# A diffusion block with two layers on one core: new costs and a new order for its instruction planner, modulation sums by narrow products, one copy less in single-group norms

## The chip, the cores and the metric

The kernel runs on one core of a Trainium2 chip: TensorE (matrix products), VectorE, ScalarE, GpSimd and SyncE (which issues all transfers here). The metric is device time in microseconds of one execution.

## What is computed

Two layers of a block with modulation on 512 latent tokens and 256 context tokens, all 1024 wide, in fp32. In each layer the six modulation vectors for the latent and the context tokens come from one 1024x6144 matrix; the mixer has three parts (neighborhood attention, latent attention, a linear recurrence), and a gated feed-forward part follows. The second layer leaves the context tokens as they are.

```python
def _adaln(cvec, w, b):
    m = jax.nn.silu(cvec) @ w + b
    return jnp.split(m[:, None, :], 6, axis=-1)
...
for l in range(DEPTH):
    sh_m, sc_m, g_m, sh_f, sc_f, g_f = _adaln(c, ada_w[l], ada_b[l])
    csh_m, csc_m, cg_m, csh_f, csc_f, cg_f = _adaln(c_ctx[None], ada_w[l], ada_b[l])
    u = _modulate(_rmsnorm(h, norm_mix_g[l]), sh_m, sc_m) @ w_in[l]
    ...
    o_lat = jnp.concatenate([na_o.reshape(B, S, NA_WIDTH), mla_o.reshape(B, S, MLA_HEADS * MLA_V), lru_o], axis=-1)
    h = h + g_m * (o_lat @ w_out[l])
    h = h + g_f * _swiglu(_modulate(_rmsnorm(h, norm_ffn_g[l]), sh_f, sc_f), ffn_w_gate[l], ffn_w_up[l], ffn_w_down[l])
```

## The kernel before

Activations lie with the feature on the partitions: eight tiles of 128 features by 768 tokens. Each fp32 product is made of three: weight and activation are split into a rounded high part and the rest (`whi`, `wlo`; tiles `s`), and high x high, high x rest and rest x high are added up in PSUM (`lin`). With 768 tokens each goes out in a piece of 512 columns and one of 256, so that one block of 128 features takes six products, "a beat" in what follows; in the second layer's feed-forward part only 512 tokens are left and a beat is three products. Weights come by `load_w` (tiles `wst`, then split). Some products stay in plain fp32; the trace has two records for each of those.

**The order.** No instruction is issued where it stands. Helpers (`mm` L497, `tr` L506, `act`, `copy` L524, `tt` L535, `ts` L541, `stt`, `scan` L1298) hand each operation to `Order.add` (L246) with a cost in ns for each engine that may do it. `Order.place` (L304) then lays all of them out greedily while the kernel is built: again and again it takes, over all engines, the operation with the earliest start by the model, ties broken by rank (its place in the program plus shifts). Waits between engines (`HOPS`), a bias for each engine (`BIAS`), a clock model for TensorE (`ClockGate`) and free buffers go into that start. The result is the static order of each engine's queue. Within a mixer the steps are listed by hand in `PLAN` (L57 on), and each has an offset on its rank after "@" (`LEAD`): a first list for layer 0, a second for layer 1. SyncE issues its transfers in that order too, and one that waits for a buffer holds back those behind it.

**Modulation.** `ada_chunks(l, ch, nv)` (L698) makes chunks of 256 columns of the modulation matrix for `nv` vectors (latent and context, or latent alone). Eight transfers of 128x256 bring the chunk's weights into `ast` tiles (three buffers). For the first vector VectorE multiplies by the vector's entry (one per partition) and accumulates in `acc` (`stt`, L570); for the second, GpSimd scales the same tile (L544) and adds it (L537). The sum over the 128 partitions is taken by TensorE: each `acc` (as moving side, 256 columns) against a block of ones with 32 columns, four sums one beside the other in four column groups; the result is copied out, and two "closing" products with a selecting matrix turn it to the partitions again. `later` gives this work a shift of `FILL_LATE`, so that it fills gaps; `od.gate` holds its transfers until the last operation before it in the list is placed. In the first layer's mixer (`ada_rest`, L895) stand 12 chunks for two vectors, in its feed-forward part (L1332) 12 more for two and 16 for one.

**Norms.** `rstd` (L647) sums squares by a product with 32 columns, moves the sums to the partitions by transposes, raises them to the power of -1/2 on GpSimd (L670, tile `rn`), copies the results out to 128 columns a tile (`rb`) and transposes that back to PSUM, where VectorE reads it. It is called with one group (the whole width) in `norm_stat`, `latent_kv`, `latent_rope` and `latent_q`, and with two in `near_k`, `near_q`, `latent_k` and `latent_query`.

In the trace the first mixer lies at about 80 to 490 us, the first feed-forward part to about 1085, the second mixer at about 1125 to 1440 and the second feed-forward part from 1480 on.

## Time and profile before

| | us |
|---|---|
| three runs: median (lowest to highest) | 1846.58 (1841.27 to 1848.17) |
| profiled execution, its own time | 1840.35 |
| its span, first to last instruction | 1838.3 |
| TensorE busy | 1773.1 |
| VectorE busy | 1100.5 |
| GpSimd busy | 725.2 |
| ScalarE busy | 481.4 |

In the rows, PE is TensorE's products, PEld its weight loads, DVE VectorE, ACT ScalarE, POOL GpSimd, SP SyncE. An operation is told as out<-in by tile names; a product's inputs are moving side, then weight; "128*32" is rows by columns of the weight. Products overlap in the pipeline, so the length of one says less than the distance from its start to the start of the next. Idle time stands in brackets with what ended it.

### The profile page before, as it was taken

How to read it: one execution, taken by the hardware profiler on the slowest of the kernel's cores; microseconds unless marked ns; L12 is line 12 of the kernel's file. 1: busy time of each engine (PE TensorE's matmuls, PEld its weight loads, DVE VectorE, ACT ScalarE, POOL GpSimd, SP SyncE). 2: the span in 40 equal slices, each digit the busy share in tenths (PEclk: the TensorE clock that was granted, in tenths of full speed). 3: DMA queues.
4: the chain of work that ended last, by engine and by line, in shares of the span. 5: the costliest groups of instructions: out<-in, count | busy, mean ns of one | idle time of the engine just before them, and what ended most of it. 6: DMA issues, size and time to landing. Idle time of an engine off the chain costs nothing.

```text
span 1838.3 us, 25772 instructions
## 1 busy us (share of the span) xinstructions
PE 1773.1 (96%) x9880; PEld 1411.0 (77%) x9880; DVE 1100.5 (60%) x1850; ACT 481.4 (26%) x912; POOL 725.2 (39%) x698
## 2 busy tenths in 40 slices
PE   8999998899989999999999999999999999999999
PEld 4777765667778888888888887777677878888787
DVE  7765478897576566566634357676876644343443
ACT  4454264663130000000000013654664210000000
POOL 2333467777537766310121022335453122232322
PEclk9999999999999999999999999999999999999999
DMA  8111111224223343444422131111101223323233
GB/s 312 52 53 46 35 50 56 92 93 129 71 94 112 112 125 116 137 153 160 142 78 70 52 109 59 62 53 53 59 24 44 72 89 94 98 86 104 81 99 96
DMA packets 86380, 166.53 MB, mean 91 GB/s; under 512 B 9968, under 2 KB 51312, under 8 KB 86256
## 3 DMA queue, kind: packets, MB, share of 16 engines
q1 hardware_dynamic: 86256, 164.88, 28.3%
q8 instruction: 78, 1.28, 0.3%
q14 instruction: 46, 0.38, 0.1%
HBM read 160.65 MB, written 4.19 MB: 90 GB/s over the span
## 4 chain that ended last, share of the span: by engine, by line
PE 77%; DVE 11%; POOL 3%; issue 3%; DMA 3%; ACT 2%; SPq 0%; DVEq 0%; POOLq 0%; ACTq 0%
PE A L502 62%; PE B L502 10%; PE B L507 4%; DMA ast<-in_ada_dram 2%; DVE acc L570 2%; DVE s L537 1%; POOL rn L670 1%; DVE s L529 1%; DVE wlo L537 1%; POOL acc L537 1%; ACT lo L516 1%; DVE lo L570 1%; DVE whi L529 1%; DVE lo L1300 1%; DVE tmp L537 1%
## 5 line engine op out<-in xcount | busy, mean ns | idle before, releaser
L502 PE MATMUL A<-s,whi 128*128 128x512 f32 (+1 forms) x4340 | 1144.8, 355 | 8.3 <-DVE s L537 2.7
L502 PEld LDWEIGHTS A<-s,whi 128*128 128x128 f32 x4340 | 759.8, 189 | 160.4 <-issue 16.6
L502 PE MATMUL A<-s,wlo 128*128 128x512 f32 (+1 forms) x2138 | 735.7, 354 | 0.1
L502 PEld LDWEIGHTS A<-s,wlo 128*128 128x128 f32 x2138 | 395.9, 189 | 58.0 <-issue 8.0
L529 DVE CAST whi<-wst 128x1024 fp32r<-128x1024 f32 (+2 forms) x183 | 125.8, 688 | 407.4 <-PE A L502 355.6
L537 POOL TENSOR_TENSOR wlo<-wst,whi 128x640 fp32r<-128x640 f32 (+2 forms) x75 | 143.8, 1917 | 428.4 <-DVE whi L529 365.7
L570 DVE SCALAR_TENSOR_TENSOR acc<-ast,cc,acc 128x256 f32<-128x256 f32 x280 | 177.7, 635 | 99.7 <-DMA ast<-in_ada_dram 96.8
L516 ACT ACTIVATE tmp<-A 128x768 f32<-128x768 f32 (+1 forms) x75 | 55.2, 735 | 535.8 <-PE A L502 530.6
L537 DVE TENSOR_TENSOR wlo<-wst,whi 128x1024 fp32r<-128x1024 f32 (+2 forms) x133 | 164.0, 1233 | 6.9 <-POOL whi L531 1.9
L670 POOL TENSOR_TENSOR rn<-rn,con 128x12 f32<-128x12 f32 (+4 forms) x44 | 84.5, 1921 | 181.1 <-DVE rn L544 174.0
L537 POOL TENSOR_TENSOR acc<-acc,ast 128x256 f32<-128x256 f32 x168 | 139.5, 831 | 9.9
L544 POOL TENSOR_SCALAR ast<-ast,cc 128x256 f32<-128x256 f32 x168 | 108.8, 650 | 73.8 <-DVE acc L570 69.2
L502 PE MATMUL A<-s,s 128*128 128x512 f32 (+1 forms) x508 | 124.4, 353 | 13.8 <-ACT lo L516 9.2
L502 PE MATMUL B<-s,s 128*64 128x256 f32 (+2 forms) x720 | 110.6, 353 | 1.3 <-DVE s L529 1.3
L502 PEld LDWEIGHTS A<-s,s 128*128 128x128 f32 x508 | 81.0, 191 | 38.1 <-ACT lo L516 12.9
L507 PE MATMUL B<-ident,tmp 128*128 128x128 f32 (+1 forms) x480 | 78.9, 278 | 19.5 <-ACT tmp L527 11.1
L502 PE MATMUL B<-s,whi 128*128 128x512 f32 (+1 forms) x364 | 93.4, 344 | 0.0
L507 PEld LDWEIGHTS B<-ident,tmp 128*128 128x128 f32 (+1 forms) x480 | 56.6, 142 | 42.3 <-ACT tmp L527 13.4
L502 PEld LDWEIGHTS B<-s,s 128*64 128x64 f32 (+1 forms) x720 | 59.2, 144 | 28.4 <-issue 13.2
L531 POOL TENSOR_SCALAR s<-tmp 128x512 fp32r<-128x512 f32 (+2 forms) x24 | 29.5, 1229 | 127.0 <-DVE tmp L537 114.0
L527 ACT COPY s<-B 128x384 f32<-128x384 f32 (+2 forms) x149 | 67.5, 472 | 38.7 <-PE B L507 35.4
L531 POOL TENSOR_SCALAR whi<-wst 128x1024 fp32r<-128x1024 f32 (+4 forms) x24 | 25.5, 1064 | 122.0 <-PE A L502 73.9
(171 smaller groups left out, 1760.5 us busy)
## 6 DMA issues: line engine op xcount, KB each, us to landing
ast<-in_ada_dram SPq DMA_DIRECT2D x320, 128.0 KB, 2.1
wst<-in_wg_dram SPq DMA_DIRECT2D x44, 512.0 KB, 3.5
wst<-in_wu_dram SPq DMA_DIRECT2D x44, 512.0 KB, 3.6
wst<-in_win_dram SPq DMA_DIRECT2D x32, 512.0 KB, 3.5
wst<-in_wd_dram SPq DMA_DIRECT2D x32, 384.0 KB, 3.1
wst<-in_wd_dram SPq DMA_DIRECT2D x32, 320.0 KB, 2.9
wst<-in_wout_dram SPq DMA_DIRECT2D x16, 512.0 KB, 3.6
hr<-in_x_dram SPq DMA_DIRECT2D x16, 384.0 KB, 3.8
```

Of the source, the lines that this page charges most:

```text
L502: od.add({"t": c / 2.4}, lambda e: nc.tensor.matmul(ap(out), lhsT=ap(lhsT), rhs=ap(rhs), start=start, stop=stop), [out], [lhsT, rhs], heat ...
L507: od.add({"t": 256 / 2.4}, lambda e: nc.tensor.transpose(ap(out), ap(in_), ap(ident)), [out], [in_, ident])
L516: nc.scalar.activation(ap(out), ap(in_), getattr(AF, func), scale=ap(scale), **kw)
L527: nc.scalar.copy(out=ap(out), in_=ap(in_))
L529: nc.vector.tensor_copy(ap(out), ap(in_))
L531: nc.gpsimd.tensor_scalar(out=ap(out), in0=ap(in_), scalar1=1.0, scalar2=1.0, op0=ALU.mult, op1=ALU.mult)
L537: (nc.vector if e == "v" else nc.gpsimd).tensor_tensor(out=ap(out), in0=ap(a), in1=ap(b), op=op)
L544: (nc.vector if e == "v" else nc.gpsimd).tensor_scalar(out=ap(out), in0=ap(a), scalar1=ap(s1), scalar2=ap(s2), op0=op0, **kw)
L570: lambda e: nc.vector.scalar_tensor_tensor(out=ap(out), in0=ap(a), scalar=ap(s), in1=ap(b), op0=op0, op1=op1),
L670: lambda e: nc.gpsimd.tensor_tensor(out=ap(r[:, :w]), in0=ap(r[:, :w]), in1=ap(C("mhalf", 0, w)), op=ALU.pow),
L1300: lambda e: nc.vector.tensor_tensor_scan(out=ap(out), data0=ap(a), data1=ap(u), initial=ap(init), op0=ALU.mult, op1=ALU.add), [out], refs( ...
```

## The change

The planner's model changes in six ways: costs of products, transposes and scans get new figures; a product whose shape differs from the one before (fp32 with fewer than 128 weight columns, or at most 64 rows, or neither) costs `SWITCH` = 95 ns and is put behind others by as much; operations of VectorE that use two inputs in SBUF or a copying mode are marked `both`, and such an operation and any of GpSimd exclude each other in the model; the bias of GpSimd goes from -274 to +600; the rule by which late work may take a PSUM buffer is loosened a little. Both mixers' lists are ordered anew. In `ada_chunks` the scaling for the second vector and the first step may go to any of three engines and the addition to VectorE or GpSimd; each `acc` is now the weight (two halves of 128 columns) against a single column of ones, two products a sum, and VectorE adds the bias straight from PSUM for each chunk. In `rstd` with one group the copy falls away: the transposes read one column of `rn` with a step of zero as a weight of 128 columns.

```diff
 PLAN, LEAD = [], {}
 for _text in ("""
-    lru_start @-26, lru_in 0 @6, lru_in 1 @18, lru_gates 1 @-5, latent_rope @-58, latent_kv @561,
...
+    near_q 1 @-103, lru_in 1 @-1458, lru_in 0 @777, latent_rope @-15, lru_gates 1, latent_kv @-21, near_k 1 @-30,
+    lru_gates 0 @-1644, latent_v, latent_k 0, lru_out 0 @2414, near_q 0 @-1471, lru_out 1 @302, latent_keys,
+    latent_q @-2498, near_v 1, lru_start, latent_k 1 @25, near_q 2 @145, near_v 0 @176, lru_scan 0 @-92,
+    ada_rest @1227, lru_scan 1 @-2483, latent_query 1 @-183, latent_put 0, near_v 2 @-2500, latent_query 0 @-2218,
...
@@ Order.place
+        shape = 0
+        port = {"v": (0.0, 0.0), "g": (0.0, 0.0)}
...
-                        if w != j and (w < 0 and not b.loose or not b.psum or len(tg.free) <= j + 1):
+                        if w != j and (w < 0 and not b.loose or not b.psum or
+                                       not b.loose and len(tg.free) <= j + 1):
...
+                    if e == "g" or e == "v" and op.both:
+                        a, b = port["v" if e == "g" else "g"]
+                        if a <= st < b:
+                            st = b
                     if op.table is not None and e == "s" and table not in op.table:
                         st_key = st + 1300.0
+                    elif e == "t" and op.shape != shape:
+                        st_key = st + SWITCH
...
             if e == "t":
+                if op.shape != shape:
+                    shape = op.shape
+                    cost += SWITCH
                 cost = clockgate.run(st, cost, op.heat)
+            if e == "g" or e == "v" and op.both:
+                port[e] = (st, st + cost)
...
+SWITCH = 95.0
...
-BIAS = {"v": -61.0, "s": 0.0, "g": -274.0, "t": 0.0, "d": 0.0}
+BIAS = {"v": -61.0, "s": 0.0, "g": 600.0, "t": 0.0, "d": 0.0}
@@ mm, tr, scan
-        c = 4 * max(out.n, 128) if f32 else max(out.n, 256)
-        if out.p[0] and lhsT.n < P:
-            c = 128
-        c += 6
-        od.add({"t": c / 2.4}, lambda e: nc.tensor.matmul(ap(out), lhsT=ap(lhsT), rhs=ap(rhs), start=start, stop=stop),
+        k, m = rhs.p[1] - rhs.p[0], lhsT.n
+        c = 0.4453 * (4 * max(out.n, 126) if f32 else max(out.n, 256)) + 3.5
+        if out.p[0] and m < P:
+            c = 25.0
+        shape = 1 if f32 and m < P else 2 if k <= 64 else 0
...
-        od.add({"t": 256 / 2.4}, lambda e: nc.tensor.transpose(ap(out), ap(in_), ap(ident)), [out], [in_, ident])
+        od.add({"t": 109.0}, lambda e: nc.tensor.transpose(ap(out), ap(in_), ap(ident)), [out], [in_, ident])
...
-        od.add({"v": 1.04 * out.n + 65},
+        od.add({"v": 2.08 * out.n + 50},
@@ scale_rows becomes scaled, with an output of its own and a list of engines
+    def scaled(out, x, r, engs="svg"):
...
@@ rstd
-        rb = f3()
-        g = rows // groups
-        copy(rb[:, : nt * rows].rearrange("p (t g) -> p t g", g=g), r[:, :w].spread(g), "vs")
+        if groups > 1:
+            rb, g = f3(), rows // groups
+            copy(rb[:, : nt * rows].rearrange("p (t g) -> p t g", g=g), r[:, :w].spread(g), "vs")
         for o, k, ps in tiles:
             for t in range(o // P, (o + k) // P):
-                tr(ps[:rows, t * P - o : (t + 1) * P - o], rb[:, t * rows : (t + 1) * rows], ident)
+                x = r[:, t].spread(rows) if groups == 1 else rb[:, t * rows : (t + 1) * rows]
+                tr(ps[:rows, t * P - o : (t + 1) * P - o], x, ident)
@@ ada_chunks
-        n = 4 // nv
-        accs = []
-        for c in range(n):
+        for c in range(ch, ch + 4 // nv):
             acc = [buf("acc", [P, 256]) for _ in range(nv)]
...
                     if kt == 0:
-                        ts(acc[v], st, w, ALU.mult, 1.0, ALU.mult, "vg"[v])
+                        scaled(acc[v], st, w)
                     elif v == 0:
                         stt(acc[v], st, w, acc[v], ALU.mult, ALU.add)
                     else:
-                        ts(st, st, w, ALU.mult, 1.0, ALU.mult, "g")
-                        tt(acc[v], acc[v], st, ALU.add, "g")
-            accs += acc
-        p = ps1()
-        for g, acc in enumerate(accs):
-            mm(p[32 * g : 32 * g + 32, :256], C("ones"), acc, True, True, f32=True)
-        r = buf("acc", [P, 256])
-        copy(r, p[:, :256], "sv")
-        q = p[:, 256:]
-        for j in range(2):
-            mm(q[:, 4 * j : 4 * j + 4], r[:, j * P : (j + 1) * P], C("sel4"), True, True, f32=True)
...
+                        scaled(st, st, w)
+                        tt(acc[v], acc[v], st, ALU.add)
+            q = ps1()[:, : 2 * nv].rearrange("p (j v) -> p j v", v=nv)
+            for v in range(nv):
+                for j in range(2):
+                    mm(q[:, j, v : v + 1], acc[v][:, j * P : (j + 1) * P], C("ones", 0, 1), True, True, f32=True)
+            tt(mods[l][:, :nv, 2 * c : 2 * c + 2].rearrange("p v j -> p j v"), q, vec(l, "adab", 2 * c, 2).spread(nv),
+               ALU.add, "v")
```

## Rows read from the trace of the kernel before

**Rows 1.** The page, part 1: busy us, share of span, instructions.

```profile
PE 1773.1 (96%) x9880; PEld 1411.0 (77%) x9880; DVE 1100.5 (60%) x1850; ACT 481.4 (26%) x912; POOL 725.2 (39%) x698
```

**Rows 2.** Busy time by stretch: length, engines (instructions), granted clock, DMA share, GB/s.

```profile
80.00:280.00 200.00, 191.33 (x1143) 149.58 (x1143) 112.78 (x164) 91.75 (x148) 93.50 (x70) 1.00 0.15 46
280.00:440.00 160.00, 141.29 (x927) 97.89 (x926) 141.85 (x305) 94.33 (x237) 121.84 (x151) 0.98 0.29 90
...
490.00:530.00 40.00, 35.33 (x215) 29.13 (x215) 28.00 (x53) 15.05 (x30) 7.32 (x7) 0.91 0.13 41
530.00:931.00 401.00, 399.76 (x2249) 333.60 (x2247) 247.25 (x384) 28.04 (x39) 174.44 (x204) 1.00 0.42 131
...
1125.00:1440.00 315.00, 303.78 (x1881) 236.51 (x1880) 214.06 (x363) 160.11 (x299) 134.17 (x110) 0.99 0.17 53
1440.00:1480.00 40.00, 35.16 (x255) 31.86 (x254) 29.20 (x58) 14.62 (x32) 8.94 (x6) 0.96 0.19 57
```

**Rows 3.** Timeline of TensorE, first layer's feed-forward: start us, length us, operation.

```profile
573.45 0.51 PE L502 MATMUL A<-s,whi 128*128 128x512 f32 x2
573.80 0.39 PE L502 MATMUL A<-s,wlo 128*128 128x512 f32 x1
...
574.50 0.51 PE L502 MATMUL A<-s,whi 128*128 128x512 f32 x2
574.95 0.62 PE L502 MATMUL B<-acc,con 128*32 128x256 f32 x4
...
576.30 0.39 PE L502 MATMUL A<-s,whi 128*128 128x512 f32 x1
576.53 0.50 PE L502 MATMUL B<-con,acc 128*128 128x4 f32 x4
...
578.86 0.52 PE L502 MATMUL A<-s,whi 128*128 128x512 f32 x2
```

**Rows 4.** The same view, around a batch with one sum.

```profile
902.22 0.28 PE L502 MATMUL A<-s,wlo 128*128 128x256 f32 x1
902.43 0.62 PE L502 MATMUL B<-acc,con 128*32 128x256 f32 x2
902.98 0.74 PE L502 MATMUL A<-s,whi 128*128 128x512 f32 x3
```

**Rows 5.** Instructions that touch tile "ast": duration ns min/median/max, first and last start.

```profile
L570 DVE SCALAR_TENSOR_TENSOR acc<-ast,cc,acc x280: 461/485/2230, 243.8 to 926.9; 128x256 f32<-128x256 f32 x140
L544 POOL TENSOR_SCALAR ast<-ast,cc x168: 467/479/1901, 244.4 to 749.9; 128x256 f32<-128x256 f32 x168
L537 POOL TENSOR_TENSOR acc<-acc,ast x168: 714/737/1732, 245.0 to 751.3; 128x256 f32<-128x256 f32 x168
L544 DVE TENSOR_SCALAR acc<-ast,cc x40: 335/353/2477, 243.5 to 919.2; 128x256 f32<-128x256 f32 x40
```

**Rows 6.** 280 to 440 us: chain of waits; groups, busy us, mean ns.

```profile
by line: PE B L502 23.1%; PE B L507 12.3%; issue 11.1%; PE A L502 9.8%; DVE acc L570 9.6%; POOL acc L537 4.5%; DVE sm L588 4.1%; DVE s L529 4.0%; DMA ast<-in_ada_dram 2.8%; DVE s L537 2.4%; DVE tmp L1295 2.3%; POOL s L537 2.3%; ACT lo L516 
...
L570 DVE SCALAR_TENSOR_TENSOR acc<-ast,cc,acc 128x256 f32<-128x256 f32 x56 | 38.9, 694 | 0.6 <-DMA ast<-in_ada_dram 0.5
...
L537 POOL TENSOR_TENSOR acc<-acc,ast 128x256 f32<-128x256 f32 x56 | 47.7, 853 | 2.8
L544 POOL TENSOR_SCALAR ast<-ast,cc 128x256 f32<-128x256 f32 x54 | 31.9, 594 | 24.7 <-DVE acc L570 20.6 <-DVE sm L585 3.0 <-POOL ast L544 0.5
```

**Rows 7.** Groups by form over the span: count, busy us, mean ns of one.

```profile
L537 DVE TENSOR_TENSOR lo<-lo,B 128x256 f32<-128x256 f32 x30 | 12.4, 412 | 12.6 <-ACT lo L527 12.5
...
L516 ACT ACTIVATE s<-tmp,mod 128x256 fp32r<-128x256 f32 x24 | 11.7, 506 | 6.3 <-DVE tmp L570 6.2
```

**Rows 8.** Timeline of all engines at the last norm before the second feed-forward part.

```profile
1459.47 0.71 POOL L670 TENSOR_TENSOR rn<-rn,con 128x2 f32<-128x2 f32 x1 [1.96 <-DVE rn L544]
1460.21 0.40 ACT L527 COPY tmp<-rn 128x256 f32<-128x256 f32 x1 [1.54 <-POOL rn L670]
...
1460.67 0.69 PE L507 MATMUL B<-ident,tmp 128*128 128x128 f32 x2 [1.68 <-ACT tmp L527]
```

More of the change, by code (lines that the diff above doesn't have):

```diff
@@ L211 @@
     __slots__ = ("i", "emit", "cost", "deps", "outs", "ndep", "rank", "bufs", "new", "table", "ready", "start", "end",
-                 "eng", "heat", "pe", "middle")
+                 "eng", "heat", "pe", "middle", "shape", "both")
 class ClockGate:
@@ L244, in __init__, with add @@
         self.shift, self.lead, self.gate = 0, 0, None
-    def add(self, cost, emit, writes, reads, table=None, heat=1.0, middle=False):
+    def add(self, cost, emit, writes, reads, table=None, heat=1.0, middle=False, shape=0, both=False):
         op = Op()
-        op.heat, op.pe, op.middle = heat, "t" in cost, middle
+        op.heat, op.pe, op.middle, op.shape, op.both = heat, "t" in cost, middle, shape, both
         op.i, op.emit, op.cost, op.table = len(self.ops), emit, cost, table
@@ L531, in go @@
                 nc.gpsimd.tensor_scalar(out=ap(out), in0=ap(in_), scalar1=1.0, scalar2=1.0, op0=ALU.mult, op1=ALU.mult)
-        od.add(costs(out.n, in_.psum, engs, 1.04 if in_.psum else 0.52, 0.835), go, [out], [in_])
+        od.add(costs(out.n, in_.psum, engs, 1.04 if in_.psum else 0.52, 0.835), go, [out], [in_], both=not in_.psum)
     def tt(out, a, b, op, engs="vg"):
@@ L537, in go @@
             (nc.vector if e == "v" else nc.gpsimd).tensor_tensor(out=ap(out), in0=ap(a), in1=ap(b), op=op)
-        od.add(costs(out.n, a.psum or b.psum, engs, 1.04, 2.1), go, [out], [a, b])
+        od.add(costs(out.n, a.psum or b.psum, engs, 1.04, 2.1), go, [out], [a, b], both=not (a.psum or b.psum))
     def ts(out, a, s1, op0, s2=None, op1=None, engs="v"):
@@ L551, in ts @@
             c["g"] += 83 * len(refs(s1, s2))
-        od.add(c, go, [out], refs(a, s1, s2))
-    def scale_rows(x, r):
+        od.add(c, go, [out], refs(a, s1, s2), both=not a.psum)
+    def scaled(out, x, r, engs="svg"):
         def go(e):
             if e == "s":
-                nc.scalar.activation(ap(x), ap(x), AF.Copy, scale=ap(r))
+                nc.scalar.activation(ap(out), ap(x), AF.Copy, scale=ap(r))
             else:
-                (nc.vector if e == "v" else nc.gpsimd).tensor_scalar(out=ap(x), in0=ap(x), scalar1=ap(r), scalar2=1.0,
+                (nc.vector if e == "v" else nc.gpsimd).tensor_scalar(out=ap(out), in0=ap(x), scalar1=ap(r), scalar2=1.0,
                                                                      op0=ALU.mult, op1=ALU.mult)
-        c = costs(x.n, False, "svg", 0.52, 0.835)
-        c["s"] += 93
-        c["v"] += 60
-        c["g"] += 83
-        od.add(c, go, [x], [x, r])
+        c = costs(x.n, False, engs, 0.52, 0.835)
+        for e, k in zip("svg", (93, 60, 83)):
+            if e in c:
+                c[e] += k
+        od.add(c, go, [out], [x, r], both=True)
     def stt(out, a, s, b, op0, op1):
@@ L570, in stt @@
                lambda e: nc.vector.scalar_tensor_tensor(out=ap(out), in0=ap(a), scalar=ap(s), in1=ap(b), op0=op0, op1=op1),
-               [out], refs(a, s, b))
+               [out], refs(a, s, b), both=not (a.psum or b.psum))
     def sub(out, a, hi, engs="vg"):
@@ L581, in memset @@
         od.add({"v": 0.52 * out.n + 65, "g": 0.6 * out.n + 60},
-               lambda e: (nc.vector if e == "v" else nc.gpsimd).memset(ap(out), val), [out], [])
+               lambda e: (nc.vector if e == "v" else nc.gpsimd).memset(ap(out), val), [out], [],
+               both=True)
     def recip(out, in_):
@@ L1298, in scan @@
     def scan(out, a, u, init):
-        od.add({"v": 1.04 * out.n + 65},
+        od.add({"v": 2.08 * out.n + 50},
                lambda e: nc.vector.tensor_tensor_scan(out=ap(out), data0=ap(a), data1=ap(u), initial=ap(init),
-                                                      op0=ALU.mult, op1=ALU.add), [out], refs(a, u, init))
+                                                      op0=ALU.mult, op1=ALU.add), [out], refs(a, u, init), both=True)
     def decay(l):
```

48 lines of the change are left out of this document (20 added, 28 removed).

## The prediction

> **What bounds the kernel now.** I read the page's busy table first: TensorE is busy for 1773.1 of 1838.3 us and idle for 65.2 [rows 1]. Then the busy time by stretch, to see where the idle time lies [rows 2]. From 530 to 931 us, the first layer's feed-forward part with the modulation sums among it, TensorE is busy for 399.8 of 401 us: there only fewer or cheaper products save time. The mixers differ: idle are 8.7 us in 80 to 280, 18.7 in 280 to 440, 4.7 in 490 to 530, 11.2 in 1125 to 1440 and 4.8 in 1440 to 1480, together 48.1; the remaining 17 are the start, the other stage change and the end. In 280 to 440 VectorE is busy for 141.9 of 160 us and GpSimd for 121.8, and the chain of waits there gives 9.6% (15 us) to VectorE's modulation accumulation and 4.5% to GpSimd's [rows 6]. So fill work, which should lie in gaps, ends waits in the densest stretch of the mixer. The granted clock is 0.98 there and 0.91 in 490 to 530; 0.09 of 40 us at half of 2.4 GHz is 3.6 us of work lost, and every closed gap may give some of it back.
>
> **Narrow products, in the saturated stretch.** The plain beat is six products in 1.05 us (573.45 to 574.50) [rows 3]. A wide batch goes in at 574.95: the next beat begins at 576.30, 1.80 after 574.50, so it costs 0.75 us. Of this 0.10 is a delay ahead of it: two such products take 0.35 (573.45 to 573.80), and the batch begins 0.45 after 574.50. That batch held two sums (four records). A batch with one sum takes as long: 0.76 from the row before it to the row after, less that row's own 0.12, is 0.64, and 0.10 for the way back is 0.74 [rows 4]. The closing pair of selecting products begins at 576.53 in a beat that began at 576.30; two beats take 2.09, the rows show 2.56 to 578.86, so the pair costs 0.47, or 0.23 each. This pair has the form of the new products: a full 128x128 fp32 weight and a few moving columns (four; the new ones have one).
> In the code the feed-forward part holds 12 chunks for two vectors and 16 for one. Before: 28 batches x 0.75 + 10 closings x 0.47 = 25.7 us. After: (12 x 4 + 16 x 2) = 80 x 0.23 = 18.4. **-7 us**, nothing hides it, since TensorE is never idle there.
> Against this speaks the Trainium skill, TensorEngine Tiling (Array Packing), When to Use Tiling: with a small moving side one should swap the operands and use column groups, as the old code does. If four sums did share one batch, ten batches and closings would take 12.2 us and the change would lose 6. The rows show batches of one or two only, because the sums become ready apart; the sum above goes by the rows.
> In the first mixer 12 chunks stand: before 12 to 24 batches and 6 closings, 11.8 to 20.8 us; after 48 x 0.23 = 11.0. That is -1 to -10; TensorE has gaps there, I take **-3**. The copy of each group's sums from PSUM and its way there and back go too; they are not on TensorE.
>
> **The second vector's scaling and adding.** GpSimd does 168 scalings and 168 additions now, medians 0.48 and 0.74 us [rows 5]. With the new bias of +600 on GpSimd the order gives the scaling mostly to ScalarE (nearest row 0.51 us for 128x256; it is busy for 94.3 of the dense 160 us [rows 2]) and the addition to VectorE (0.41 us) [rows 7]. Load on VectorE: 168 x 0.41 = 69 us more, 56 of the adds in 280 to 440 if nothing moved (23 us). What it gets back: its 280 accumulations take 0.461 at best, 0.485 in the median and up to 2.23 us [rows 5], in 280 to 440 a mean of 0.694 [rows 6]; 56 x (0.694 - 0.485) is 12 us there that comes from working beside GpSimd. So this edit is about even for VectorE and frees GpSimd for the powers in the norms; I take **0**, with -5 and +25 as ends (the +25 is a rival).
> The Trainium skill, SBUF — State Buffer, Who interferes with whom, calls the port that both engines share an exclusive lock, held for an instruction, against VectorE's copies in fast modes and its operations with two SBUF inputs. The longest duration agrees: 2.23 us is 1.75 over the median, and the longest GpSimd addition took 1.73 [rows 5]. This is what the new model marks with "both"; if it is the rule, an order that keeps the two apart loses nothing by it.
> A wait is added: an "ast" buffer (three) is now free when ScalarE's scaling and VectorE's addition are done, no longer GpSimd's. Behind it on SP's queue stand the next modulation load and the weight loads in program order. The chain is 0.49 + 0.51 + 0.41 us instead of 0.49 + 0.48 + 0.74, so I cost it at nothing; with VectorE saturated a weight load would wait with it. The modulation loads of the first mixer now wait for a scan step in place of a projection; if they start earlier by it, that helps, as VectorE is busy for only 112.8 of 200 us in 80 to 280 [rows 2].
>
> **No spread copy in norms of one group.** 14 norms (six in the mixers, eight at the stage changes) lose a copy between the power and the transposes. At 1459 us the power ends at 1460.18, the copy takes 0.40 and the transposes start at 1460.67 [rows 8]; 0.46 goes, and more with larger tiles. At four stage changes TensorE waits on this: 4 x 0.5 = **-2**. The transposes then load weights with a zero step; no row shows such a load. Bounds: no dearer than a plain one, or once more the 0.23 us of a product with a fresh weight of 128 columns [rows 3] for some 56 transposes, +13 us at most; I take 0, as the instruction and the 128 columns are those of the plain load.
>
> **The new costs and the order on them.** The old model has a 512 and a 256 product at 215.8 and 109.2 ns, the new one at 231.5 and 117.5; three of each are 0.98 us and 1.05, the row is 1.05 [rows 3]. The shape change of 95 ns agrees with the 0.10 above. So the new model is nearer to the chip where these rows can judge it, and engine choices and mixer order follow from it. How much of the 48.1 us of idle time that gives back no row tells: bounds are two thirds (-32) and a loss as in the last rival. I take a quarter, **-12**, since the old order too was packed by the same greedy rule and much of the idle is chains of norm, softmax and value product that any order has. Of shape changes, 44 norms and 30 value steps in the code make at least 74 visits at 0.2 us, 15 us; grouping a fifth of them gives **-3**. Shorter gaps mean fewer clock drops: **-3** of some 12 us (shortfall times length: 0.02 x 160 + 0.09 x 40 + 0.01 x 315 + 0.04 x 40).
>
> **Sum.** -7 -3 +0 -2 -12 -3 -3 = -30 us. The profiled execution took 1840.35 us (span 1838.3 and 2 around it), so 1810; it lies 6.2 below the median of the runs, 1846.58, on which the same saving gives **1816.6**, rounded 1816.
>
> **Rivals.** (a) The order takes most of the gaps: -32 in place of -12 and -6 on the clock: 1846.6 - 53 = 1794. For it: all costs are corrected at once. Against: VectorE is near full in 280 to 440.
> (b) The order is worth nothing, that is, the change doesn't do what it says: GpSimd's exclusion and the shape changes were no cause of the gaps. Only sums and copies remain, -12: 1834.6, with the zero-step load at its dear end 1848. Sums that were packed by four before belong here too (+6 in place of -7, 1829 with the rest as forecast), but the rows speak against them.
> (c) **Slower: VectorE becomes the bound in the first mixer.** In 280 to 440 it has 18 us free. If the 56 additions stay there (23), the scalings go to it as well (54 at 0.35 [rows 5] is 19) and three quarters of GpSimd's other 42 us (121.8 less the 47.7 and 31.9 of [rows 6]) move at half their price (16), with no relief of durations, it has 58 us more and 40 too many; less the -12 of (b) that is +28: 1875. With half the scalings on ScalarE and the relief of 12 it is 40 - 10 - 12 = 18 too many; with only the -7 to set against it +11: 1857, and this milder form is the likelier. It decides when VectorE's load in the dense stretch passes its length.
>
> **How the numbers follow.** Forecast 0.48 (own range 1800 to 1830), (a) 0.17, (b) 0.21, (c) 0.14. The range 1787 to 1850 leaves out about 0.1 below, where (a) goes further, and 0.1 above, where most of (c) lies. A change of 0.5% (9 us) is about what a measurement of this kernel can tell: faster by more than that is the forecast, (a) and a third of (b), 0.73; within it the rest of (b) and a little of (c), 0.15; slower 0.12.
>
> **What would show it.** Sums: no 32-column batches on "acc", about 256 records of the narrow form (two each) at 0.11, TensorE still full in 530 to 931, and this stretch's work some 7 us shorter. GpSimd far under 121.8 us in 280 to 440, VectorE's accumulations near 0.49, ScalarE's total up by 60 to 90 us. Order: idle TensorE time in the two mixers near 36 in place of 48. Wrong: VectorE over 0.95 busy in a stretch where TensorE waits for its "acc" or "s" tiles; two transposes after the power taking far more than the 0.69 of [rows 8]; SP held up ahead of weight loads.

## The result, and the profile after

The change is slower by 0.7%: 1857.82 us (1854.2 to 1865.88) against 1845.07 us, ratio 1.0074 with an interval of 1.0052 to 1.0095. The forecast of 1816 had the wrong sign, and the range to 1850 did not hold the time. The traced execution took 1865.88 us, the longest of its six.

The page of the changed kernel, parts 1 and 2, answers [rows 1]:

```profile
PE 1758.0 (94%) x9944; PEld 1447.7 (78%) x9944; DVE 1160.0 (62%) x2116; ACT 564.1 (30%) x1042; POOL 347.9 (19%) x282
...
PEclk9999989998999999999999999999999999999999
```

GpSimd has lost half of its work, as meant, and TensorE 15 us of busy time. Yet the span grew from 1838.3 to 1864.1 us: TensorE is idle for 106.1 us instead of 65.2. The "8"s in the clock line are new too: the line of before has forty "9"s. In the trace of before the granted clock is at 1.2 instead of 2.4 GHz in 6 pieces with 30.7 us in all, in this one in 20 pieces with 95.6 us.

The stretches of [rows 2] in the changed kernel (length, busy us of PE, PEld, DVE, ACT, POOL, granted clock, DMA share, GB/s):

```profile
80.00:280.00 200.00, 171.47 (x977) 138.95 (x977) 132.45 (x216) 94.64 (x140) 82.01 (x53) 0.93 0.21 66
280.00:440.00 160.00, 140.30 (x1020) 112.11 (x1019) 152.27 (x354) 112.11 (x275) 78.69 (x81) 0.97 0.25 78
...
530.00:931.00 401.00, 390.73 (x2229) 338.61 (x2229) 271.59 (x520) 73.28 (x116) 36.06 (x23) 0.98 0.42 129
1125.00:1440.00 315.00, 290.36 (x1841) 233.20 (x1841) 219.78 (x387) 171.80 (x315) 126.41 (x100) 0.96 0.16 49
```

In 80 to 280 TensorE was idle for 8.7 us before and is for 28.5 now, at a clock of 0.93. The saturated stretch, 530 to 931, is saturated no longer: 10.3 us idle instead of 1.2. VectorE has 152.27 of 160 us in the dense stretch.

The order moved the work, so stretches of equal time no longer hold equal work. The table below cuts each trace at the start of the last output addition of each part (VectorE's operation hr<-B,mod,hr; in the last part hr<-A,mod,hr), with TensorE's idle time within it and, as "clock", the shortfall of the granted clock times the length. The rows with a_ are runs of the changed kernel with one edit, those with b_ runs of the kernel before with one or two (a_again has none); they are explained further down. One execution each: the first feed-forward part of the changed kernel differs by 2.7 us between two executions, and the first mixer, whose queues are the same in before and b_narrow_ffn, by 5.6 us between these two.

| | start and first mixer | idle, clock | first feed-forward | idle, clock | second mixer | idle, clock | rest |
|---|---|---|---|---|---|---|---|
| before | 509.1 | 37.4, 5.1 | 592.9 | 5.1, 3.4 | 354.9 | 14.9, 5.1 | 377.8 |
| after | 519.3 | 58.9, 25.6 | 605.0 | 14.5, 10.2 | 358.3 | 25.1, 11.9 | 377.8 |
| a_again | 519.7 | 59.3, 25.6 | 602.3 | 15.7, 5.1 | 354.9 | 25.9, 6.8 | 378.2 |
| b_narrow_ffn | 514.7 | 37.7, 10.2 | 586.8 | 6.1, 3.4 | 358.0 | 15.5, 8.5 | 378.1 |
| a_pool_ffn | 519.1 | | 591.4 | 8.1, 5.1 | 355.9 | 24.9, 10.2 | 381.3 |
| a_true_ffn | 518.0 | | 598.4 | 13.3, 5.1 | 360.4 | | 377.8 |
| a_wide_ffn | 520.1 | | 598.8 | 11.9, 8.5 | 354.7 | | 381.2 |
| a_null1 | 510.7 | 53.9, 25.6 | 604.0 | 14.3, 10.2 | 359.1 | 25.7, 11.9 | 379.8 |
| a_noswitch | 536.8 | 62.9, 25.6 | 606.9 | | 370.7 | 29.1, 10.2 | 378.3 |
| a_pe93 | 540.9 | 73.5, 42.7 | 595.8 | | 382.6 | 39.7, 23.9 | 381.4 |
| a_gp_back | 533.7 | 68.8, 37.5 | 612.7 | 20.2 | 371.3 | 33.4 | 378.6 |
| a_noport | 524.5 | 65.5 | 604.7 | | 369.3 | 32.3 | 377.9 |
| a_bias_back | 509.6 | 55.0, 23.9 | 600.5 | | 373.1 | 35.2, 18.8 | 378.2 |
| a_eng_back | 511.4 | 52.9 | 596.7 | | 372.2 | 31.9, 22.2 | 378.2 |
| b_null1 | 537.1 | 52.5, 18.8 | 592.3 | 4.4 | 362.5 | 21.5 | 379.0 |
| b_rstd | 541.9 | 55.5, 22.2 | 593.9 | | 368.8 | 27.0 | 377.2 |
| b_newmm | 548.3 | 56.1, 30.7 | 601.9 | | 369.5 | 27.0 | 377.3 |
| b_newplan | 542.8 | 57.9, 27.3 | 595.0 | | 380.3 | 37.2 | 378.1 |
| b_copy_held | 505.1 | 34.5, 3.4 | 594.0 | 5.4, 3.4 | 352.3 | 14.1, 3.4 | 377.6 |
| b_both_held | 504.0 | 37.5, 5.1 | 588.3 | 5.8, 5.1 | 355.3 | 15.2, 5.1 | 377.6 |

So the loss lies in the first mixer (+10 us in these two traces; +5 against b_narrow_ffn, which has the queues of before there) and in the first feed-forward part (+9 to +12), where the forecast had gains in both. Two causes were possible in each: the edits themselves, or the order that the planner makes of them.

The new products, in the timeline of TensorE of the changed kernel (start, length, operation, idle time before it and its releaser), beside [rows 3]:

```profile
576.28 0.28 PE L517 MATMUL A<-s,wlo 128*128 128x256 f32 x1
577.12 0.61 PE L517 MATMUL B<-con,acc 128*128 128x1 f32 x4 [0.56 <-DVE acc L586]
577.59 0.60 PE L517 MATMUL A<-s,whi 128*128 128x512 f32 x2
578.04 0.61 PE L517 MATMUL B<-con,acc 128*128 128x1 f32 x4
578.51 0.48 PE L517 MATMUL A<-s,wlo 128*128 128x512 f32 x1
...
713.06 0.58 PE L517 MATMUL B<-con,acc 128*128 128x1 f32 x4 [1.88 <-DVE acc L586]
713.50 1.13 PE L517 MATMUL A<-s,whi 128*128 128x512 f32 x3
714.43 0.63 PE L517 MATMUL A<-s,wlo 128*128 128x512 f32 x1
```

Where its operand is ready, one sum (two products, four records, at 578.04) holds TensorE from 578.04 to 578.51, 0.47 us or 0.23 a product, the price of the prediction. But at 577.12 and 713.06 TensorE has first stood idle for 0.56 and 1.88 us until VectorE's accumulation was done. At 713.8 the clock falls to half for 3.4 us: the 512 product at 714.43 takes 0.63 instead of 0.39 us [rows 3].

Tile "ast" in the changed kernel (count, duration ns min/median/max, first and last start) answers [rows 5] and [rows 7]; [rows 4] have no answer, since no 32-column batch on "acc" is left:

```profile
L586 DVE SCALAR_TENSOR_TENSOR acc<-ast,cc,acc x280: 459/482/2202, 179.1 to 893.3; 128x256 f32<-128x256 f32 x140
L552 DVE TENSOR_TENSOR acc<-acc,ast x123: 405/421/2011, 199.5 to 729.2; 128x256 f32<-128x256 f32 x123
L573 ACT ACTIVATE ast<-ast,cc x89: 492/509/523, 187.9 to 727.0; 128x256 f32<-128x256 f32 x89
L575 DVE TENSOR_SCALAR ast<-ast,cc x71: 338/353/1934, 200.4 to 728.7; 128x256 f32<-128x256 f32 x71
L552 POOL TENSOR_TENSOR acc<-acc,ast x45: 725/737/1647, 181.6 to 727.7; 128x256 f32<-128x256 f32 x45
```

The medians are those of the prediction (0.42 for the addition, 0.51 on ScalarE). 123 of 168 additions went to VectorE. The longest are as long as before, 2.0 to 2.2 us. The addition of 2.01 us starts at 654.55, beside a subtraction that occupies GpSimd from 654.44 to 656.29: the model's exclusion did not always keep the two engines apart on the chip. In 280 to 440, though, the accumulations got the relief that the prediction hoped for, from the mean of 694 ns in [rows 6] to 564 (group by form, with count, busy us, mean ns):

```profile
L586 DVE SCALAR_TENSOR_TENSOR acc<-ast,cc,acc 128x256 f32<-128x256 f32 x49 | 27.6, 564 | 1.2 <-DMA ast<-in_ada_dram 1.1
```

### The profile page after: what moved, and what is told of

Same layout as the page of the kernel before. It is cut to its first block, busy times and chain, and to the rows that moved or that the text cites. A ratio compares the mean times of both kernels' runs of the same rounds, so it can differ in the third digit from the quotient of the medians.

```text
span 1864.1 us, 25692 instructions
## 1 busy us (share of the span) xinstructions
PE 1758.0 (94%) x9944; PEld 1447.7 (78%) x9944; DVE 1160.0 (62%) x2116; ACT 564.1 (30%) x1042; POOL 347.9 (19%) x282
## 5 line engine op out<-in xcount | busy, mean ns | idle before, releaser
L544 DVE CAST whi<-wst 128x1024 fp32r<-128x1024 f32 (+2 forms) x179 | 115.6, 646 | 425.1 <-PE A L517 410.4
L552 DVE TENSOR_TENSOR wlo<-wst,whi 128x1024 fp32r<-128x1024 f32 (+2 forms) x189 | 212.5, 1125 | 6.0 <-ACT whi L542 0.9
L586 DVE SCALAR_TENSOR_TENSOR acc<-ast,cc,acc 128x256 f32<-128x256 f32 x280 | 156.3, 559 | 78.0 <-DMA ast<-in_ada_dram 76.0
L542 ACT CAST s<-tmp 128x768 fp32r<-128x768 f32 (+2 forms) x57 | 42.4, 744 | 271.8 <-DVE tmp L552 258.6
L517 PE MATMUL B<-s,s 128*64 128x256 f32 (+2 forms) x720 | 88.4, 352 | 1.1 <-DVE lo L552 0.7
L522 PE MATMUL B<-ident,tmp 128*128 128x128 f32 (+1 forms) x424 | 68.0, 283 | 17.6 <-ACT tmp L542 11.5
L552 POOL TENSOR_TENSOR wlo<-wst,whi 128x1024 fp32r<-128x1024 f32 (+2 forms) x19 | 43.6, 2297 | 217.5 <-DVE whi L544 123.2
L573 ACT ACTIVATE ast<-ast,cc 128x256 f32<-128x256 f32 x89 | 45.1, 508 | 122.9 <-DVE acc L586 114.0
L586 DVE SCALAR_TENSOR_TENSOR hr<-A,mod,hr 128x512 f32<-128x512 f32 x105 | 69.0, 658 | 7.4 <-PE A L517 7.3
L531 ACT ACTIVATE tmp<-hr 128x256 f32<-128x256 f32 (+1 forms) x64 | 30.3, 495 | 130.5 <-DVE hr L586 120.9
```

The lines of the kernel that those rows point to most:

```text
L517: od.add({"t": c}, lambda e: nc.tensor.matmul(ap(out), lhsT=ap(lhsT), rhs=ap(rhs), start=start, stop=stop), [out], [lhsT, rhs], heat=0.5 i ...
L522: od.add({"t": 109.0}, lambda e: nc.tensor.transpose(ap(out), ap(in_), ap(ident)), [out], [in_, ident])
L531: nc.scalar.activation(ap(out), ap(in_), getattr(AF, func), scale=ap(scale), **kw)
L542: nc.scalar.copy(out=ap(out), in_=ap(in_))
L544: nc.vector.tensor_copy(ap(out), ap(in_))
L552: (nc.vector if e == "v" else nc.gpsimd).tensor_tensor(out=ap(out), in0=ap(a), in1=ap(b), op=op)
```

## Experiments: the first feed-forward part

Theory A: the narrow products are cheap, but stand in TensorE's queue before VectorE has their sums ready. Theory B: the products themselves lower the clock. Theory C: GpSimd beside VectorE costs more than it frees.

**b_narrow_ffn**: the kernel before, with the narrow products in the first feed-forward part only; the second vector stays on GpSimd.

```diff
+    def ada_ffn(l, ch, nv):            # called in the first feed-forward part
...
+                        ts(st, st, w, ALU.mult, 1.0, ALU.mult, "g")
+                        tt(acc[v], acc[v], st, ALU.add, "g")
+            for v in range(nv):
+                for j in range(2):
+                    mm(q[:, j, v : v + 1], acc[v][:, j * P : (j + 1) * P], C("ones", 0, 1), True, True, f32=True)
```

> The kernel before, with the narrow products in the first feed-forward part alone; mixers and start keep their planned order. From the last addition of the first mixer's output to the last of the feed-forward part the kernel before takes 592.9 us (509.1 to 1102.0 in its trace), the changed one 605.0 (519.3 to 1124.3). Theory A (the narrow products are cheap, what costs is that they stand in TensorE's queue before VectorE has their sums ready, after the work moved to VectorE): 592.9 - 7 = 586, clock 1.00 within the stretch 560 to 930. Theory B (the narrow products by themselves let the granted clock fall): 593 to 600, with drops in that stretch as in the changed kernel (0.92, 0.82 at 680 to 720).

1841.05 us, ratio 0.9965 (0.9951 to 0.9979). The part went from 592.9 to 586.8 us, -6.1 where the prediction had -7, with the clock as before. Theory B falls. The loss of the changed kernel in this part is not in the products.

**a_pool_ffn**: the changed kernel, with the second vector back on GpSimd in this part only.

```diff
-                        scaled(st, st, w)
-                        tt(acc[v], acc[v], st, ALU.add)
+                        scaled(st, st, w, "g")
+                        tt(acc[v], acc[v], st, ALU.add, "g")
```

> The changed kernel, with the second vector's scalings and additions back on GpSimd in the first feed-forward part. Theory A (VectorE's load makes the sums late): the part falls to 605 - 13 = 592 or, with the cheap products in full, 586. Theory B: drops stay, about 600. Rival C (work on GpSimd beside VectorE costs more than it frees): not under 605, with VectorE's accumulations back at a mean of 0.63 us from 0.56.

1853.96 us, ratio 1.005 (1.0032 to 1.0068). The part takes 591.4 instead of 602 to 605 us; by the time of the whole run the gain is smaller, 4 to 9 us (1.005 against 1.0074 and, for the changed kernel once more, 1.0098). TensorE's waits in 530 to 931 us (waited for: us in total, times, longest), first of the changed kernel:

```profile
PE B L517 <- DVE acc L586: 9.2, 11, 1.9
```

and with the second vector on GpSimd:

```profile
PE B L517 <- DVE acc L586: 3.3, 2, 2.0
```

Eleven waits become two. Theory C falls here: GpSimd was slow, but its 0.48 + 0.74 us lay beside everything, while 0.42 us on VectorE stand in the queue that the sums wait in.

**a_true_ffn**: the changed kernel; in this part the planner gets costs nearer to the chip's means (`stt` 560, `tt` 465, scaling 410 on VectorE and 508 ns on ScalarE).

> The changed kernel, with the durations that its trace shows for the modulation work (accumulation 0.560 us in place of 0.391, addition 0.465 for 0.331, scaling 0.410 on VectorE and 0.508 on ScalarE for 0.258 and 0.398) given to the planner for the first feed-forward part; the first mixer is unchanged. Theory A: TensorE's 9.7 us of waits for acc in this part shrink to under 4, the clock drops at 666, 697 and 714 us go, and the part takes 605 - 6 - 6 = 593 or less. Theory B: waits shrink, the drops stay, 605 - 5 = 600.

1859.79 us, ratio 1.0072 (1.0056 to 1.0087): no gain in the median, and 598.4 us for the part. TensorE's waits for `acc` shrink from 9.2 to 4.0 us, as expected, but 3.9 us of waits for `hr` stand beside them (1.2 in the changed kernel). Costs alone do not take the waits away.

**a_wide_ffn**: the changed kernel with the old wide batches and closings in this part.

> The changed kernel, with the old wide sums (one batch of 32 columns a sum, closings) in the first feed-forward part, engines as in the changed kernel. Theory A: the late sums hold TensorE up as before, the wide batches cost 7 us more: 605 + 7 = 612, drops stay. Theory B: the drops go, 605 + 7 - 8 = 604, clock 1.00 in 640 to 720.

1860.26 us, ratio 1.0072 (1.0047 to 1.0096); 598.8 us. Under the old engines wide batches cost 6 us more than narrow products; under the new ones nothing, and the trace has less idle time (11.9 us). This part of theory A missed; why late sums hurt a wide batch less was not settled.

## Experiments: the model's pieces, one at a time

Theory S: grouping by shape makes TensorE wait. M: the old, too short product costs acted as a margin. G: work taken from GpSimd makes VectorE the late engine in the mixers, too. P: the new costs and lists lose the mixers. L: the lists with their offsets fit one exact order, and any edit throws that away, on the chip too. Q: the old order is as good in any near variant. C is as above. What each would give stands in the expectations.

**a_again**: the changed kernel once more, beside the others.

> The changed kernel itself once more, since the traced execution was the slowest of its six. All theories: 1858 us by median, granted clock 0.975 to 0.98, first mixer with start about 519 us, first feed-forward part 598 to 605, second mixer about 358.

1865.91 us, ratio 1.0098 (1.0077 to 1.0118).

**a_noswitch**: no price for a change of shape.

```diff
-SWITCH = 95.0
+SWITCH = 0.0
```

> The changed kernel with the price of a shape change set to 0, so that products are no longer gathered by shape (the planner itself expects 25 us more). Theory S (gathering the 32 and 64 column fp32 products makes TensorE wait and lets the clock fall): idle TensorE time in the first mixer falls from 59 towards 40 us and in the second from 25 towards 15, the clock rises from 0.975 to 0.985, time 1845 to 1850 although shape changes rise again. Theory M (the planner now has TensorE right and the other engines 13 to 17% too fast, so TensorE comes to each product before its input): no gain, idle time as before, 1858 to 1875 with the changes paid.

1899.51 us, ratio 1.0283 (1.0268 to 1.0298). Shape changes, counted from one product to the next in the trace (fewer than 128 weight columns, at most 64 rows, or neither), are 166 from 80 to 515 us and 133 from 1110 to 1470 before, 70 and 64 in the changed kernel, 124 and 94 here. S falls: without grouping the mixers are 17 and 12 to 16 us longer.

**a_pe93**: all of TensorE's costs times 0.93, back to about the old level (231.5 x 0.93 is 215.3 ns).

> The changed kernel with all of TensorE's costs multiplied by 0.93 in the placing, which brings back the old too short products (215.8 for 231.5 ns) and with them the old relation to the other engines. Theory M: idle TensorE time falls from 59 to about 45 us in the first mixer with start and from 25 to about 15 in the second, clock 0.985, time 1845 to 1850. Theory S: no change, 1858 or, as offsets are not made for it, up to 1870.

1902.39 us, ratio 1.0298 (1.0277 to 1.0319). M falls: the idle time grows to 73.5 and 39.7 us. Both runs are slower than any theory had them.

**a_gp_back**: the old bias, no exclusion, and the second vector back on GpSimd everywhere. **a_eng_back**: the same with the exclusion kept. **a_bias_back** and **a_noport**: the bias alone, the exclusion alone.

```diff
-BIAS = {"v": -61.0, "s": 0.0, "g": 600.0, "t": 0.0, "d": 0.0}
+BIAS = {"v": -61.0, "s": 0.0, "g": -274.0, "t": 0.0, "d": 0.0}
...
-                    if e == "g" or e == "v" and op.both:
+                    if False:
                         a, b = port["v" if e == "g" else "g"]
```

> The changed kernel with all of its GpSimd part undone: second vector's modulation work on GpSimd, its bias -274 again, no exclusion in the placing. Shape changes, new product and scan costs, narrow products, norms without the copy and both new lists stay. Theory G (work taken from GpSimd makes VectorE the engine that TensorE waits for, everywhere): first feed-forward part 605 to 587 as with the narrow products alone, idle TensorE time of the first mixer with start from 59 to about 40, clock up, 1835 to 1843 by median. Theory P (the new lists and the new product costs lose the time in the mixers): first mixer stays at 511 to 520 and the second at 355 to 359, only the feed-forward part gains, 1845 to 1852.

> The changed kernel with the second vector's work on GpSimd and the bias at -274, the exclusion kept. Against the full undoing this shows what the exclusion gives where GpSimd has its work: Theory G with a true exclusion: 3 to 8 us better than the full undoing, 1830 to 1840. If the exclusion is of no use since the chip's times drift from the plan: the same within 4 us. Theory P: 1845 to 1852.

> The changed kernel with GpSimd's bias back at -274 and nothing else undone: more splits and modulation work go to GpSimd where the planner has a choice, the exclusion stays. Theory G: half of the gain of the full undoing, 1848 to 1853, first feed-forward part 592 to 598. Theory P: mixers as they are, 1853 to 1858. Rival C (GpSimd beside VectorE costs more than it frees): slower than 1862.

> The changed kernel without the exclusion of VectorE and GpSimd in the placing, bias and engines as in the changed one. Rival C: VectorE's accumulations go from a mean of 0.56 us towards 0.63 and the time up by 5 to 15, 1865 to 1875. Theory G: exclusion matters little beside the bias, 1855 to 1865.

1899.37 us, ratio 1.0286 (1.027 to 1.0302); 1856.29, 1.005 (1.0034 to 1.0066); 1865.28, 1.01 (1.0082 to 1.0117); 1883.55, 1.0205 (1.0183 to 1.0228). Taking the exclusion away costs about 20 us by itself (1.0205 against 1.0098) and 43 with the old engines (a_gp_back against a_eng_back). The engines and the bias of before, with the exclusion, give a first mixer of 511.4 and a second of 372.2 us: no gain in sum. G falls for the mixers.

Three of the four lie in the range of no theory. a_bias_back lies in that of C (over 1862), but so does the changed kernel without an edit at 1865.91, so it decides nothing.

No single piece is shown to be the cause; under the new lists a piece is worth 20 to 43 us, or nothing, and since each of these edits also makes a new order, such a figure is not the price of the piece alone. P is not settled by them. That left the fit itself.

## Experiments: an edit, and the order it makes

**a_null1** and **b_null1**: the changed kernel and the kernel before, with an edit that means nothing, the weight of the rank's second term.

```diff
-BLEND = 0.0633
+BLEND = 0.0643
```

> The changed kernel with one weight of the planner's tie-break moved from 0.0633 to 0.0643, which means nothing but gives another order with offsets that were not made for it (the planner itself expects 11 us more). If the offsets carry the time: 1858 + 11 = 1869. If the planner's small differences don't reach the chip: within 5 us of 1858.

> The kernel before with the tie-break weight moved from 0.0633 to 0.0643, which means nothing; its planner expects 33 us more. Theory L (the old lists carry the time: their offsets fit this one order, and any edit of the planner throws that fit away, on the chip too): 1846 + 15 to 33 = 1861 to 1879, lost in the two mixers, feed-forward parts as before. Theory Q (the old order is as good in any near variant, the new one is worse by its own making): 1843 to 1853.

The changed kernel takes 1861.49 us, ratio 1.0081 (1.0064 to 1.0098), as without the edit: its offsets carry no such time. The kernel before takes 1875.07, ratio 1.0155 (1.0132 to 1.0179): 1.5% lost to an edit that changes no operation. Its dense stretch (columns as in the stretches above):

```profile
280.00:440.00 160.00, 131.32 (x784) 89.90 (x783) 125.16 (x272) 83.87 (x202) 108.37 (x148) 0.89 0.26 78
```

All engines do less there than in [rows 2], at a clock of 0.89 instead of 0.98, and none is near full. That the same work no longer interlocks is the reading of this; no single wait shows it. Q falls, and L holds for the kernel before, by one such edit.

**b_rstd**, **b_newmm**, **b_newplan**: one part of the change alone put into the kernel before: the missing copy in norms of one group, the new costs of products, the new lists.

> The kernel before without the spread copy in norms of one group, everything else as it was; its planner expects 37 us more since the offsets no longer fit. The copy by itself is worth -2 (stage changes). Theory L: 1858 to 1880. Theory Q: 1840 to 1846.

> The kernel before with the new costs of products and transposes alone (0.4453 ns a column and 3.5, 109 for a transpose). Theory M on this side (the old, too short products kept a margin for the other engines): idle TensorE time in the first mixer with start from 36 to 50 us and more. Theory L: 1861 to 1880 like any other edit. If true costs help by themselves: under 1846.

> The kernel before with the new lists and offsets of both mixers and nothing else of the change; its planner expects 59 us more. Theory L: 1880 to 1905, as the lists fit the new model alone. If the new lists are better in themselves: 1830 to 1846.

1889.41 us, ratio 1.0233 (1.0212 to 1.0254); 1902.64, 1.0307 (1.0286 to 1.0328); 1900.19, 1.0294 (1.0265 to 1.0323). All lose 43 to 56 us, most of it in the mixers; the first two lose more than L had (up to 1880). b_null1 makes some 29 us by a new order alone likely in each, but that is one draw, and what the new costs and lists cost beyond it is not separated. Whether the missing copy itself had a part was open.

**b_copy_held**: the kernel before without that copy, in the order of before. The planner still lays out the copy, so every queue keeps its order; it is only not issued. (In the trace the queues of all engines are those of before less the 14 copies.)

```diff
-        copy(rb[:, : nt * rows]..., r[:, :w].spread(g), "vs")
+        if groups > 1:
+            copy(rb[:, : nt * rows]..., r[:, :w].spread(g), "vs")
+        else:
+            od.add(costs(nt * rows, False, "vs", 0.52, 0.835), lambda e: None, [rb[:, : nt * rows]], [r[:, :w]])
...
+                    od.add({"t": 256 / 2.4}, lambda e, out=out, y=r[:, t].spread(rows):
+                           nc.tensor.transpose(ap(out), ap(y), ap(ident)), [out], [x, r[:, :w], ident])
```

> The kernel before without the copy in norms of one group; the planner still lays out the copy and the transposes as before, so that the order of every queue and the choice of every engine stay, and only the 14 copies are not issued. Theory L (the loss of 43 us in the run that dropped the same copy and let the planner lay all out anew is the new order, not the edit): the edit alone is worth the 2 us of the prediction, at most 7 (14 norms x 0.46): 1839 to 1845, the first mixer's part at 507 to 509 us, the second's at 353 to 355. Rival N (the transposes that read one column with a step of zero, or what waits for them, cost by themselves): over 1850, and if all of the loss were theirs, 1880 to 1890 with the first mixer's part at about 540.

1841.26 us (1834.74 to 1844.29), ratio 0.9969 (0.9958 to 0.998): 5.3 us faster than the kernel before beside it, where the same edit with a new order lost 43. The norm of [rows 8] in its timeline:

```profile
1454.02 0.71 POOL L670 TENSOR_TENSOR rn<-rn,con 128x2 f32<-128x2 f32 x1 [1.96 <-DVE rn L544]
...
1454.78 0.43 PE L685 MATMUL B<-ident,rn 128*128 128x128 f32 x2 [1.20 <-POOL rn L670]
```

The transposes start 0.05 us after the power, not 0.49, and the pair takes 0.43 us at a granted clock of 1.00. (The 0.69 of [rows 8] were taken in a piece at half clock, from 1460.1 to 1463.5, which the prediction did not note.) N falls, and by this pair of runs the new order of b_rstd cost some 48 us by itself.

**b_both_held**: the same, and each sum as two narrow products where its wide product stood; the copy of the sums and the closing pair are laid out and not issued.

```diff
+            def two(e, g=g, acc=acc):
+                for j in range(2):
+                    nc.tensor.matmul(ap(q[:, 4 * j + g : 4 * j + g + 1]), lhsT=ap(acc[:, j * P : (j + 1) * P]),
+                                     rhs=ap(C("ones", 0, 1)), start=True, stop=True)
+            od.add({"t": (134 if g else 1030) / 2.4}, two, [p[32 * g : 32 * g + 32, :256]], [C("ones"), acc])
```

> The same, and each sum of the modulation goes out as two narrow products at the place where its wide product stood, with the copy and the closing pair not issued; the second vector's work stays on GpSimd, the order of every queue is that of before. Theory L: this is the -12 of the prediction's rival (b), -7 in the first feed-forward part, -3 in the first mixer, -2 in the norms: 1832 to 1838, the feed-forward part at 585 to 588 us, the first mixer's at 503 to 508. Rival F (the saving needs an order laid out for it; put in the old places the narrow products stand where nothing was freed for them): the feed-forward part at 591 or more and the time within 3 us of the other kernel of this pair.

**1829.78 us** (1824.42 to 1832.01), ratio 0.9907 (0.9892 to 0.9922): 16.8 us faster than before, a little more than L had (1832 to 1838), and some 30 faster than the changed kernel, each against the kernel before beside it. F falls: the feed-forward part is 588.3 us. Its page and its stretch from 530 to 931 us:

```profile
PE 1762.9 (96%) x9944; PEld 1427.0 (78%) x9944; DVE 1092.4 (60%) x1842; ACT 473.3 (26%) x890; POOL 729.1 (40%) x698
...
530.00:931.00 401.00, 398.58 (x2315) 348.42 (x2314) 246.81 (x390) 22.21 (x27) 176.57 (x205) 1.00 0.44 132
```

TensorE has the 9944 products of the changed kernel, ten microseconds less busy time than before, and is idle for 65.9 us in place of 65.2. So the two edits that remove work were worth about 17 us. The rest of the change, the second vector's engines, the new model and the new lists, cost about 30 (12.8 + 16.8), by this difference.

## Why the prediction was wrong, point by point

**What bounds the kernel**: right, and it carried the two terms that held.

**Narrow products, -7 and -3**: right in sum. In the feed-forward part -6.1 with its own order and -5.7 in the held one (588.3 against 594.0); the trace of before has 29 wide batches there, not 28. The difference of the two held kernels' medians, 11.5 us, is all that the narrow products gave, against 10 forecast. The -3 in the first mixer is not shown by itself: TensorE's busy time falls by 4.1 us in the held traces (470.6 to 466.5), its idle time grows by 3.0, and the part goes from 505.1 to 504.0.

**No copy, -2**: the sign right, too small. 5.3 us in the held order, where the prediction counted the four stage changes alone. In the traced execution, the fastest of its nine, the mixers are shorter (505.1 for 509.1, 352.3 for 354.9), but parts vary by as much, so where the other 3 us come from is open. The zero-step load costs as a plain one: its 56 take 0.106 to 0.232 us with a median of 0.136; the 480 transposing loads from `tmp` of before have a median of 0.140.

**The second vector's work, 0**: this step failed in size, and in place. It was weighed in 280 to 440, where relief and load were to cancel; the price fell due where TensorE has no other gap. In the first feed-forward part it is about 11 to 14 us by the traces (602 to 605 against 591.4) and 4 to 9 by the runs' times, with the wait that rival (c) names, but not where (c) put it. 1857 as (c)'s mild form is a coincidence of the time, not its mechanism: its condition, VectorE's load over the length of 280 to 440, did not come about. The sign of being wrong that the prediction gave, VectorE over 0.95, is just reached there (152.27 of 160), but TensorE waits there for VectorE's "acc" and "s" tiles for 2.1 us (3.7 before), does more products (1020 records instead of 927), and its idle time is 19.7 us instead of 18.7.

**The order, -12, -3 and -3**: this step failed in sign, and it is the larger one. Idle time in the two mixers was to fall by 12 us; in the table's first and second mixer columns, start included, it grows from 52.3 to 84.0. Of the 30 us above, 16 or more are left for the new model and lists when the 4 to 14 of the second vector are taken off; that is a difference, no run shows it by itself. Its two reasons were that the new costs are nearer to the chip and that the old order was packed by the same greedy rule. Both are true, and neither says that the new order is better: the offsets of the old lists belong to one exact order. b_null1 shows what the rule without fitting offsets gives, 1875 us. So the changed kernel is about 9 to 17 us better than the kernel before with an edit that means nothing (1857.82 and 1865.91 against 1875.07), which is no more than the work removed is worth, and 12.8 worse than the kernel before as it stood. The prediction had no rival for that: (b), "the order is worth nothing", took zero as the worst, and (c) has the loss from VectorE's load.

The shape changes did become fewer (166 to 70, 133 to 64), and TensorE's busy time in the first mixer's part fell from 471.7 (509.1 - 37.4) to 460.4 us, or 6.1 less than in the held kernel (466.5), in spite of the lower clock. The idle time took more back: 58.9 us instead of 37.5. TensorE's waits from 30 to 515 us in the changed kernel (as above) begin with

```profile
PE A L517 <- ACT lo L531: 10.0, 8, 3.2
PE B L522 <- ACT tmp L542: 9.4, 7, 6.3
PE B L522 <- DVE rb L544: 8.2, 6, 3.6
PE A L517 <- POOL wlo L552: 4.6, 1, 4.6
```

The last three have 4.6, 1.6 and 0 us before. Two of them in the timeline of the changed kernel:

```profile
159.28 2.38 POOL L552 TENSOR_TENSOR s<-tmp,s 64x768 fp32r<-64x768 f32 x1
161.63 2.98 POOL L687 TENSOR_TENSOR rn<-rn,con 128x12 f32<-128x12 f32 x1
164.64 0.83 ACT L542 COPY tmp<-rn 128x768 f32<-128x768 f32 x1 [4.35 <-POOL rn L687]
165.53 1.54 PE L522 MATMUL B<-ident,tmp 128*128 128x128 f32 x6 [6.30 <-ACT tmp L542]
...
181.21 3.01 DVE L1309 TENSOR_TENSOR_SCAN lo<-lo,s 128x256 f32<-128x256 f32 x2
182.57 3.78 POOL L552 TENSOR_TENSOR wlo<-wst,whi 128x1024 fp32r<-128x1024 f32 x1
184.15 3.29 DVE L1309 TENSOR_TENSOR_SCAN lo<-lo,lo,s 128x512 f32<-128x512 f32 x1
186.41 1.44 PE L517 MATMUL A<-s,wlo 128*128 128x512 f32 x3 [4.60 <-POOL wlo L552]
```

A norm with two groups keeps its copy: power, copy and transposes follow one another while TensorE stands for 6.30 us with nothing else next in its queue, and the clock is at half from 164.3 to 171.1. At 182.57 GpSimd's subtraction and VectorE's scans, which the model excludes from one another, run side by side, and TensorE waits 4.60 us for the result; the subtraction takes 3.78 us, where the median of the 11 of this form is 2.40. So the plan's times and the chip's had drifted apart by then. That this drift makes the remaining gaps as a whole is only argued; an order made with the chip's own durations was not run.

**The clock, -3**: wrong sign, as with the idle time: 20 pieces at 1.2 GHz with 95.6 us instead of 6 with 30.7. With the three gaps shown, of 6.30, 4.60 and 1.88 us, come pieces from 164.3, 184.8 and 713.8 on.

## What to carry to other kernels

Where the order comes from a rule with fitted offsets, an edit has two prices, the work that it removes and the new order; the second was 29 us for one edit of nothing to the kernel before and none for the same edit to the changed kernel, against 17 for all that was saved. Lay the removed operations out still and do not issue them: the order holds, and the edit is measured, and had, by itself. Before work is moved off a slow engine, ask whether the full engine waits for the one that gets it: here 0.74 us on GpSimd left two waits for the sums, 0.42 us on VectorE eleven.

## What was not expected of the hardware

An operation that shares time with another engine's can be far over its median: a 128x256 addition on VectorE has a median of 0.42 and a longest of 2.01 us. This agrees with the exclusive lock that the Trainium skill, SBUF — State Buffer, Who interferes with whom, describes: the longest ran beside a GpSimd subtraction of 1.84 us. What no row of before told is that of a 512-column scan and a 128x1024 subtraction side by side both get longer, 3.29 us for 1.26 at the shortest and 3.78 for a median of 2.40. One sum as two products with a single moving column takes 0.47 us, where one wide batch took 0.75 us whether it held one sum or two, and a closing pair for each group of four 0.47 more.
